# The third block pair of an FFN's up projection: its transposes directly behind the early products

## The chip, the cores and the metric

The kernel runs on one core of a Trainium2 chip. The metric is device time in microseconds (us) of one execution; lower is better. The program is a whole forward pass: four layers, one launch.

## The reference

A trunk of four layers on an input of 256 tokens x 1024 channels, all in float32. Each layer is a token mixer (kinds A, B, C, A) and then a gated FFN with a causal convolution over three tokens; each of the two is normed before and after and added to the residual. Cut to what matters here:

```python
def conv_ffn(h, w_up, conv_w, conv_b, w_down):
    u = h @ w_up                                   # 256 x 1024 by 1024 x 5632
    up = jnp.pad(u, ((0, 0), (CONV_WIDTH - 1, 0), (0, 0)))
    c = conv_b + up[:, CONV_WIDTH - 1:] * conv_w[CONV_WIDTH - 1]
    for j in range(CONV_WIDTH - 1):
        c = c + up[:, j:j + S] * conv_w[j]
    gate, val = jnp.split(c, 2, axis=-1)           # 2816 columns each
    return (jax.nn.gelu(gate, approximate=True) * val) @ w_down

def reference(x, ...):
    h = x
    for i in range(DEPTH):
        y = mixer_of_kind(i % 3)(rms_norm(h, g[0]))
        h = h + rms_norm(y, g[1])
        y = conv_ffn(rms_norm(h, g[2]), ...)
        h = h + rms_norm(y, g[3])
    return h
```

## The kernel before

**Products.** Every float32 operand is split into a rounded high part and a rest, and each product is made of three TensorE matmuls (`mm3`, lines 315 to 317): high x high, high x rest, rest x high. The weights come in units of 128 x 1024 values. `next_unit` takes one: SyncE starts its DMA into a `raw` tile (four buffers), ScalarE (ACT) copies it to the high part `wh` (line 277), VectorE (DVE) subtracts to give the rest `wl` (line 278). There are six `wh`/`wl` buffers, so ACT and DVE run up to six units ahead of TensorE (PE) and then wait for PE to be done with a buffer.

**The up projection of the FFN.** `w_up` is cut into 22 pairs of column blocks (`NFF`), the i-th pair being 128 gate columns and the 128 value columns that belong to them. One pair is two units. What is wanted in PSUM for a pair is columns on the partitions and tokens along the row, 128 x 256 for the gate and the same for the value, because the convolution then is a shift along the row.

- Pairs 3 to 21 are made that way directly by `proj`: the weights are the stationary operand, the transposed activations `yT` the moving one, 24 matmuls of 256 columns for each unit.
- Pairs 0 to 2 are made early and the other way round (`early`, line 459), since the first 128 tokens of `yT` are there before the last 128: `yT` is stationary, the weights move, and the result has tokens on the partitions. For the first token half, then for the second: pairs 0 and 1 go into the tile `early` (512 columns), ACT copies it to SBUF (`tok`, line 470), and pair 2 goes into the tile `more`, which the trace calls `up`. Behind the last product of the half, PE turns `tok` with four 128 x 128 transposes (line 474) into the tiles of pairs 0 and 1. Between the halves stands `late()`, eight transposes of the second token half (`zT`, line 429).
- `turn` (line 476) does the rest for pair 2: ACT copies `more` to a `tok` tile of its own (line 481), and PE turns it with four transposes (line 486) into a tile `turn`.

`activate` (its first instruction is line 1205, on ACT) does convolution, gelu and product of a pair, ACT and DVE alternating. It runs behind the products: it is recorded when more than three pairs wait in the list `behind`.

**What sets the order.** Each engine runs its instructions in a fixed order. A scheduler makes it from its own estimate of times, keeping to data dependences and to `issue_after(x)`, which makes what is recorded inside it stand behind x on the engine's queue. In `early`, `issue_after(last)` puts the four transposes somewhere behind the last early product of the half; in `ffn`, `turn` is called after the first unit of pair 3 and its transposes stand behind that unit's last product. `early` and `turn` are also used in mixers B and C, through `proj_pair`, with other blocks behind them. A wait of an engine is decided by semaphores when the instruction is at the head of its queue: everything behind it on that engine waits too.

Of the kernel before, what the change touches and what calls it, by code (L numbers as in the profile page):

```python
# [19 lines left out]
P = 128  # L20
D = 1024
KB = D // P
S = 256
# [203 lines left out]
class Trunk:  # L227
# [231 lines left out]
    def early(self, yT, outs, late, more):  # L459


        nc = self.nc
        units = [self.next_unit() for _ in range(6)]
        both = [self.ps_ot(f"early{self.unit}_{t}") for t in range(2)]
        for t in range(2):
            if t == 1:
                late()
            self.proj_tok(TILES[t], both[t], yT, units[:4], 2)
            tok = self.work.tile([P, 512], F32, tag="z", bufs=2, name=f"tok{self.unit}_{t}")
            nc.scalar.activation(tok, both[t], AF.Copy)  # L470
            last = self.proj_tok(TILES[t], more[:, t * S : (t + 1) * S], yT, units[4:])
            with self.tc.issue_after(last.ins):
                for n in range(4):
                    nc.tensor.transpose(outs[n][:, t * P : (t + 1) * P], tok[:, n * P : (n + 1) * P], self.ident)

    def turn(self, more, n, after):

        nc = self.nc
        tok = self.work.tile([P, 512], F32, tag="z", bufs=2, name=f"tok{self.unit}")
        tok = tok[:, : 2 * n * P].rearrange("p (t n) -> p t n", t=2)  # L480
        nc.scalar.activation(tok, more.rearrange("p (t n) -> p t n", t=2)[:, :, : n * P], AF.Copy)
        out = self.ps_tr(f"turn{self.unit}")
        with self.tc.issue_after(after.ins):
            for t in range(2):
                for j in range(n):
                    nc.tensor.transpose(out[:, j * S + t * P : j * S + (t + 1) * P], tok[:, t, j * P : (j + 1) * P], self.ident)
        return out

    def rows_mm(self, y, xT, unit, half, start, stop):
# [704 lines left out]
    def ffn(self, yT, L, finish, late):  # L1194
        nc = self.nc
        with self.tc.tile_pool(name="ffn", bufs=1) as fp:
# [3 lines left out]
            def activate(i, ps):  # L1200
                c = fp.tile([P, 2, S], F32, tag="c", bufs=2, name=f"c{L}_{i}")
                for j in range(2):
                    u = ps[:, j * S : (j + 1) * S]
                    w = [cw[:, i, j, k : k + 1] for k in range(4)]
                    nc.scalar.activation(c[:, j], u, AF.Identity, bias=w[3], scale=w[2])  # L1205
                    for k in (1, 0):
                        n = 2 - k
                        nc.vector.scalar_tensor_tensor(  # L1208
                            c[:, j, n:], in0=u[:, : S - n], scalar=w[k], in1=c[:, j, n:], op0=ALU.mult, op1=ALU.add
                        )  # L1210
                g = fp.tile([P, S], F32, tag="g", bufs=2, name=f"g{L}_{i}")
                nc.scalar.activation(g, c[:, 0], AF.Gelu_apprx_tanh)
                nc.vector.tensor_tensor(g, g, c[:, 1], op=ALU.mult)
                self.split(act[0][:, i], act[1][:, i], g)

            tiles = [self.ps_mm(f"up{L}_{i}") for i in range(2)]
            more = self.ps_one(f"up{L}_2")
            self.early(yT, [x[:, j * S : (j + 1) * S] for x in tiles for j in range(2)], late, more)
            self.prefetch(fp)
            behind = [(i, tiles[i]) for i in range(2)]  # L1220
            for i in range(3, NFF):
                ps = (self.ps_tr, self.ps_one, self.ps_ot, self.ps_ot, self.ps_mm, self.ps_mm, self.ps_tr, self.ps_tr)[i - 3 if i < 5 else 2 + (i - 5) % 6](f"up{L}_{i}")
                for j in range(2):
                    last = self.proj(ps[:, j * S : (j + 1) * S], yT, self.next_unit())
                    if i == 3 and j == 0:
                        behind.append((2, self.turn(more, 2, last)))
                behind.append((i, ps))
                while len(behind) > ACT_LAG:
                    activate(*behind.pop(0))
# [4 lines left out]
            def part(t, k, unit, half):  # L1234
                x = [a[:, k, t * P : (t + 1) * P] for a in act]
                return self.rows_mm(y[t], x, unit, half, k == 0, k == NFF - 1)
# [7 lines left out]
            for t in range(2):  # L1244
                with ExitStack() as ctx:
                    if t == 1:
                        ctx.enter_context(self.tc.issue_after(last.ins))
                    for k, half in halves(0, HOLD):
                        if t == 1 and k == HOLD - TAIL and half == 0 and self.turned:
                            ctx.enter_context(self.tc.issue_after(self.turned.ins))  # L1250
                        last = part(t, NFF - HOLD + k, units[k], half)
# [105 lines left out]
```

## Time and profile before

| | us |
|---|---|
| runs of before | 1600.68, 1596.98, 1599.86 |
| their median | 1599.86 |
| the profiled execution | 1599.39 |
| its span | 1597.6 |

| engine | busy us | share of the span | instructions |
|---|---|---|---|
| PE (matmul) | 1549.1 | 97% | 11016 |
| PEld (weight load) | 1444.8 | 90% | 11016 |
| DVE | 1213.1 | 76% | 2151 |
| ACT | 978.5 | 61% | 1707 |
| POOL | 252.7 | 16% | 310 |

The span is the time from the first to the last instruction of the profiled execution; its own time, 1599.39, lies 1.8 us above the span and 0.47 below the median. The mean granted clock of TensorE is 0.986 of its full speed. PE and PEld are two halves of one engine: the weight load of the next product runs beside the current product. Products overlap each other too, so a busy share of PE counts time in which at least one is under way, and the speed of PE is read from the distance between the starts of two products rather than from the duration of one.

### The profile page before, as it was taken

What the parts mean: (1) busy time and instruction counts of PE and PEld (TensorE: products, weight loads), DVE (VectorE), ACT (ScalarE), POOL (GpSimd) and SP (SyncE); (2) the same over time, 40 slices, a digit from 0 to 9 for tenths busy, and PEclk for the clock granted to TensorE, in tenths of its full rate; (3) what the DMA queues carried; (4) which work ended last, traced back from release to release, by engine and by line L of the source; (5) the groups of instructions that cost most, each with busy time, mean ns of one, the idle gap of its engine ahead of it and who ended that gap; (6) DMA issues with size and microseconds to landing.
All of it is one profiled execution on the core that took longest, in us unless ns stands there. A gap on an engine that the chain in (4) does not pass through costs nothing.

```text
span 1597.6 us, 29196 instructions
## 1 busy us (share of the span) xinstructions
PE 1549.1 (97%) x11016; PEld 1444.8 (90%) x11016; DVE 1213.1 (76%) x2151; ACT 978.5 (61%) x1707; POOL 252.7 (16%) x310
## 2 busy tenths in 40 slices
PE   7999999899999899999997999999999999899998
PEld 6999999799988789998886789988999999799986
DVE  5787898698856868885688679876587889779863
ACT  5566666476645847664567667655566666667642
POOL 2433321000001610000113200000443322000000
PEclk9999999899999999999997999999999999999999
DMA  7665556366574536557553066666556665556652
GB/s 259 198 183 180 181 183 204 122 217 189 177 238 144 146 110 221 187 171 246 170 185 101 10 202 192 188 186 211 171 178 187 180 183 178 167 185 195 187 189 79
DMA packets 103724, 282.73 MB, mean 177 GB/s; under 512 B 10928, under 2 KB 40112, under 8 KB 103584
## 3 DMA queue, kind: packets, MB, share of 16 engines
q1 hardware_dynamic: 101376, 272.86, 54.8%
q0 software_dynamic: 2208, 8.01, 1.5%
q8 instruction: 87, 1.43, 0.4%
q14 instruction: 53, 0.43, 0.1%
HBM read 279.66 MB, written 1.16 MB: 176 GB/s over the span
## 4 chain that ended last, share of the span: by engine, by line
PE 85%; DVE 5%; issue 4%; ACT 3%; DMA 2%; POOL 1%; SPq 0%; DVEq 0%; POOLq 0%; ACTq 0%
PE up L315 10%; PE up L317 9%; PE up L316 9%; PE qk L315 5%; PE qk L317 5%; PE qk L316 5%; PE y_ff L315 5%; PE y_ff L317 5%; PE y_ff L316 5%; PE s L858 4%; PE v L317 3%; PE v L316 3%; PE v L315 3%; PE pT L531 2%; DMA raw<-in_weights_dram 2%
## 5 line engine op out<-in xcount | busy, mean ns | idle before, releaser
L277 ACT ACTIVATE wh<-raw 128x1024 fp32r<-128x1024 f32 x473 | 495.5, 1057 | 357.2 <-PE up L316 124.1
L278 DVE TENSOR_TENSOR wl<-raw,wh 128x1024 fp32r<-128x1024 f32 x433 | 534.1, 1242 | 169.5 <-ACT wh L277 167.1
L315 PE MATMUL up<-yT,wh 128*128 128x256 f32 x1216 | 340.4, 280 | 0.0
L316 PE MATMUL up<-yT,wh 128*128 128x256 f32 x1216 | 339.9, 280 | 0.0
L317 PE MATMUL up<-yT,wl 128*128 128x256 f32 x1216 | 339.3, 279 | 0.0
L317 PEld LDWEIGHTS up<-yT,wl 128*128 128x128 f32 x1216 | 228.6, 188 | 0.0
L315 PEld LDWEIGHTS up<-yT,wh 128*128 128x128 f32 x1216 | 228.3, 188 | 0.0
L316 PEld LDWEIGHTS up<-yT,wh 128*128 128x128 f32 x1216 | 227.4, 187 | 0.0
L315 PE MATMUL qk<-yT,wh 128*128 128x256 f32 x768 | 216.1, 281 | 0.0
L316 PE MATMUL qk<-yT,wh 128*128 128x256 f32 x768 | 215.9, 281 | 0.0
L317 PE MATMUL qk<-yT,wl 128*128 128x256 f32 x768 | 215.8, 281 | 0.0
L1208 DVE SCALAR_TENSOR_TENSOR c<-up,cw,c 128x255 f32<-128x255 f32 x336 | 156.2, 477 | 5.1 <-ACT c L1205 2.5
L315 PEld LDWEIGHTS qk<-yT,wh 128*128 128x128 f32 x768 | 144.8, 188 | 2.3 <-issue 1.5
L316 PEld LDWEIGHTS qk<-yT,wh 128*128 128x128 f32 x768 | 144.8, 189 | 1.6 <-issue 0.7
L317 PEld LDWEIGHTS qk<-yT,wl 128*128 128x128 f32 x768 | 144.6, 188 | 1.5 <-issue 0.7
L315 PE MATMUL y_ff<-wh,act 128*128 128x512 f32 x352 | 138.1, 394 | 0.0
L317 PE MATMUL y_ff<-wh,act 128*128 128x512 f32 x352 | 138.0, 392 | 0.0
L376 POOL TENSOR_TENSOR r_post<-v_post,neg_half 128x1 f32<-128x1 f32 x16 | 8.9, 554 | 811.5 <-DVE v_post L374 811.5
L316 PE MATMUL y_ff<-wl,act 128*128 128x512 f32 x352 | 136.8, 389 | 0.0
L278 POOL TENSOR_TENSOR wl<-raw,wh 128x1024 fp32r<-128x1024 f32 x40 | 97.7, 2442 | 174.7 <-ACT wh L277 143.4
L315 PE MATMUL v<-wh,yT 128*128 128x256 f32 x400 | 113.7, 286 | 0.3 <-ACT yT L432 0.2
L316 PE MATMUL v<-wl,yT 128*128 128x256 f32 x400 | 113.7, 285 | 0.2 <-DVE wl L278 0.2
(233 smaller groups left out, 3086.8 us busy)
## 6 DMA issues: line engine op xcount, KB each, us to landing
raw<-in_weights_dram SPq DMA_DIRECT2D x473, 512.0 KB, 4.3
bias<-rows SPq DMA_DIRECT2D x160, 128.0 KB, 3.7
gain<-in_norm_gains_dram POOLq DMA_DIRECT2D x15, 512.0 KB, 4.8
out_dram<-h SPq DMA_DIRECT2D x2, 512.0 KB, 2.6
h<-in_x_dram SPq DMA_DIRECT2D x2, 256.0 KB, 3.5
gain<-in_norm_gains_dram SPq DMA_DIRECT2D x1, 512.0 KB, 5.7
h<-in_x_dram SPq DMA_DIRECT2D x1, 512.0 KB, 9.8
onehot<-in_onehot_dram SPq DMA_DIRECT2D x1, 448.0 KB, 11.4
```

The source lines that it names most:

```text
L277: self.nc.scalar.activation(hi, src, AF.Copy)
L278: (engine or self.nc.vector).tensor_tensor(lo, src, hi.bitcast(F32), op=ALU.subtract)
L315: mm(out, lh, rh, start=start, stop=False)
L316: mm(out, lh, rl, start=False, stop=False)
L317: return mm(out, ll, rh, start=False, stop=stop)
L376: self.p_last = nc.gpsimd.tensor_tensor(r, v, self.neg_half, op=ALU.pow)
L531: nc.tensor.transpose(ps[:, i * P : (i + 1) * P], x, self.ident)
L858: self.s_last = self.nc.tensor.matmul(out, q, k, start=start, stop=stop)
L1208: nc.vector.scalar_tensor_tensor(c[:, j, n:], in0=u[:, : S - n], scalar=w[k], in1=c[:, j, n:], op0=ALU.mult, op1=ALU.add)
```

## The change

`early` returns its last product. In `ffn`, `turn` is called right behind `early` instead of after the first unit of pair 3, so its transposes need only stand behind the last early product. `turn` keeps its last transpose, and all products of pairs 3 to 7 are put behind that transpose with `issue_after`. Mixers B and C call the same helpers as before.

```diff
--- before.py
+++ after.py
@@ -472,6 +472,7 @@
             with self.tc.issue_after(last.ins):
                 for n in range(4):
                     nc.tensor.transpose(outs[n][:, t * P : (t + 1) * P], tok[:, n * P : (n + 1) * P], self.ident)
+        return last
 
     def turn(self, more, n, after):
 
@@ -483,7 +484,7 @@
         with self.tc.issue_after(after.ins):
             for t in range(2):
                 for j in range(n):
-                    nc.tensor.transpose(out[:, j * S + t * P : j * S + (t + 1) * P], tok[:, t, j * P : (j + 1) * P], self.ident)
+                    self.turn_last = nc.tensor.transpose(out[:, j * S + t * P : j * S + (t + 1) * P], tok[:, t, j * P : (j + 1) * P], self.ident)
         return out
 
     def rows_mm(self, y, xT, unit, half, start, stop):
@@ -1215,15 +1216,17 @@
 
             tiles = [self.ps_mm(f"up{L}_{i}") for i in range(2)]
             more = self.ps_one(f"up{L}_2")
-            self.early(yT, [x[:, j * S : (j + 1) * S] for x in tiles for j in range(2)], late, more)
+            last = self.early(yT, [x[:, j * S : (j + 1) * S] for x in tiles for j in range(2)], late, more)
             self.prefetch(fp)
             behind = [(i, tiles[i]) for i in range(2)]
+            behind.append((2, self.turn(more, 2, last)))
             for i in range(3, NFF):
                 ps = (self.ps_tr, self.ps_one, self.ps_ot, self.ps_ot, self.ps_mm, self.ps_mm, self.ps_tr, self.ps_tr)[i - 3 if i < 5 else 2 + (i - 5) % 6](f"up{L}_{i}")
                 for j in range(2):
-                    last = self.proj(ps[:, j * S : (j + 1) * S], yT, self.next_unit())
-                    if i == 3 and j == 0:
-                        behind.append((2, self.turn(more, 2, last)))
+                    with ExitStack() as ctx:
+                        if i < 8:
+                            ctx.enter_context(self.tc.issue_after(self.turn_last.ins))
+                        self.proj(ps[:, j * S : (j + 1) * S], yT, self.next_unit())
                 behind.append((i, ps))
                 while len(behind) > ACT_LAG:
                     activate(*behind.pop(0))
```

Behind line 474 the lines of the changed kernel have numbers higher by one (486 is now 487, 481 is 482, 1205 is 1206).

What this does to the order of the instructions. First PE in the FFN of layer 0 before, around the end of the early products; `up_2` is the tile of pair 2, `up_3` that of pair 3, `yT` the transposed activations, `tok` ACT's copy of an early tile. Where a row of dots stands, 9 and then 16 more products of `up_3` are left out:

```order
L316 MATMUL up_2_3780<-wl_3814,yT_0_2_3662 128x256
L317 MATMUL up_2_3780<-wh_3813,yT_0_2_3663 128x256
L315 MATMUL up_3_3945<-yT_0_2_3662,wh_3948 128x256
L316 MATMUL up_3_3945<-yT_0_2_3663,wh_3948 128x256
L317 MATMUL up_3_3945<-yT_0_2_3662,wl_3949 128x256
...
L315 MATMUL up_3_3945<-yT_0_2_3662,wh_3948 128x256
L474 MATMUL up_0_3778<-ident,tok_1_3911 128x128 x2
L474 MATMUL up_1_3779<-ident,tok_1_3911 128x128 x2
L316 MATMUL up_3_3945<-yT_0_2_3663,wh_3948 128x256
...
L315 MATMUL up_3_3945<-yT_0_2_3662,wh_3985 128x256
L486 MATMUL turn_3978<-ident,tok_3976 128x128 x4
L316 MATMUL up_3_3945<-yT_0_2_3663,wh_3985 128x256
```

Before, 13 products of `up_3` stand between the last early product and the transposes of line 474, and 18 more between these and the transposes of `turn`. The same place on PE in the changed kernel:

```order
L316 MATMUL up_2_3780<-wl_3814,yT_0_2_3662 128x256
L317 MATMUL up_2_3780<-wh_3813,yT_0_2_3663 128x256
L474 MATMUL up_0_3778<-ident,tok_1_3911 128x128 x2
L474 MATMUL up_1_3779<-ident,tok_1_3911 128x128 x2
L487 MATMUL turn_3947<-ident,tok_3945 128x128 x4
L315 MATMUL up_3_3952<-yT_0_2_3662,wh_3955 128x256
L316 MATMUL up_3_3952<-yT_0_2_3663,wh_3955 128x256
L317 MATMUL up_3_3952<-yT_0_2_3662,wl_3956 128x256
```

Both groups of transposes now stand directly behind the last early product, and the 31 products stand behind both. It is the same in the FFN of all four layers. Next ACT at this place, before:

```order
L277 ACTIVATE wh_4028<-raw_4026 128x1024
L470 ACTIVATE tok_1_3911<-early_1_3818 128x512
L277 ACTIVATE wh_4058<-raw_4056 128x1024
L277 ACTIVATE wh_4101<-raw_4099 128x1024
L481 ACTIVATE tok_3976<-up_2_3780 128x512
L277 ACTIVATE wh_4131<-raw_4129 128x1024
L1205 ACTIVATE c_0_4013<-up_0_3778,cw 128x256
```

And in the changed kernel:

```order
L277 ACTIVATE wh_4028<-raw_4026 128x1024
L470 ACTIVATE tok_1_3911<-early_1_3818 128x512
L277 ACTIVATE wh_4058<-raw_4056 128x1024
L277 ACTIVATE wh_4101<-raw_4099 128x1024
L482 ACTIVATE tok_3945<-up_2_3780 128x512
L277 ACTIVATE wh_4131<-raw_4129 128x1024
L1206 ACTIVATE c_0_4013<-up_0_3778,cw 128x256
```

Nothing moved here: the copy that `turn` needs stands behind the same two weight copies. The queues of POOL and SyncE are in the same order as before. The scheduler has also moved a few products in mixers B and C, which the source does not touch; the largest such place is on PE in mixer B (`s` are scores, `pt` the turned probabilities, `ot` the product with the values, `pT` transposes of probabilities). Before:

```order
L858 MATMUL s_6_1_6607<-kd,q 128x256
L858 MATMUL s_6_1_6607<-kl,q 128x256
L858 MATMUL s_6_1_6607<-kd,q 128x256
L858 MATMUL s_6_1_6607<-kl,q 128x256
L316 MATMUL ot_2_6419<-pt_1_5858,v 128x256
L317 MATMUL ot_2_6419<-pt_0_5857,v 128x256
L315 MATMUL ot_2_6419<-pt_0_5857,v 128x256
L316 MATMUL ot_2_6419<-pt_1_5858,v 128x256
L317 MATMUL ot_2_6419<-pt_0_5857,v 128x256
L555 MATMUL pT_3_1_6504<-ident,p_3_1_6392 128x128 x3
```

In the changed kernel:

```order
L316 MATMUL ot_2_6419<-pt_1_5858,v 128x256
L317 MATMUL ot_2_6419<-pt_0_5857,v 128x256
L315 MATMUL ot_2_6419<-pt_0_5857,v 128x256
L316 MATMUL ot_2_6419<-pt_1_5858,v 128x256
L317 MATMUL ot_2_6419<-pt_0_5857,v 128x256
L556 MATMUL pT_3_1_6504<-ident,p_3_1_6392 128x128 x3
L859 MATMUL s_6_1_6607<-kd,q 128x256
L859 MATMUL s_6_1_6607<-kl,q 128x256
L859 MATMUL s_6_1_6607<-kd,q 128x256
L859 MATMUL s_6_1_6607<-kl,q 128x256
```

Four score products moved behind five products with the values and three transposes. Two more places, one in mixer B (`s_7_1`) and one in mixer C (six products of `s_3`), have moves of the same kind.

## Rows read from the trace of the kernel before

**Rows 1.** The page: span, and the chain that ended last, by engine.

```profile
span 1597.6 us, 29196 instructions
...
PE 85%; DVE 5%; issue 4%; ACT 3%; DMA 2%; POOL 1%; SPq 0%; DVEq 0%; POOLq 0%; ACTq 0%
```

**Rows 2.** Windows: us, busy and (count) of PE, PEld, DVE, ACT, POOL; clock, DMA share, GB/s.

```profile
322.00:328.00 6.00, 6.00 (x55) 6.00 (x54) 5.13 (x7) 5.54 (x8) 0.00 (x0) 1.00 0.80 276
```

**Rows 3.** Timeline of PE, layer 0: start us, duration us, engine, line, operation, out<-in, count.

```profile
322.92 0.28 PE L317 MATMUL up<-wh,yT 128*128 128x256 f32 x1
...
324.39 0.28 PE L315 MATMUL up<-yT,wh 128*128 128x256 f32 x1
324.51 0.60 PE L474 MATMUL up<-ident,tok 128*128 128x128 f32 x4
...
327.07 0.60 PE L486 MATMUL turn<-ident,tok 128*128 128x128 f32 x4
327.43 0.36 PE L316 MATMUL up<-yT,wh 128*128 128x256 f32 x1
327.63 0.28 PE L317 MATMUL up<-yT,wl 128*128 128x256 f32 x1
...
330.10 0.28 PE L317 MATMUL up<-yT,wl 128*128 128x256 f32 x1
```

**Rows 4.** Timeline of ACT, layer 0; in brackets idle time before it and its releaser.

```profile
321.81 0.60 ACT L470 ACTIVATE tok<-early 128x512 f32<-128x512 f32 x1 [0.40 <-PE early L317]
322.30 2.00 ACT L277 ACTIVATE wh<-raw 128x1024 fp32r<-128x1024 f32 x2
324.20 0.59 ACT L481 ACTIVATE tok<-up 128x512 f32<-128x512 f32 x1
```

**Rows 5.** Timelines, layer 3: the last early product on PE, and ACT's copy.

```profile
1421.50 0.28 PE L317 MATMUL up<-wh,yT 128*128 128x256 f32 x1
...
1422.78 0.59 ACT L481 ACTIVATE tok<-up 128x512 f32<-128x512 f32 x1
```

**Rows 6.** Timelines and a window: transposes and a short wait in the early part, layer 0.

```profile
312.84 0.60 PE L474 MATMUL up<-ident,tok 128*128 128x128 f32 x4
313.28 1.04 PE L429 MATMUL zT<-ident,z_pre 128*128 128x128 f32 x8
314.56 0.50 PE L315 MATMUL early<-wh,yT 128*128 128x512 f32 x1 [0.25 <-ACT yT L432]
...
312.00:316.00 4.00, 3.75 (x28) 3.34 (x27) 2.25 (x4) 1.09 (x2) 1.10 (x2) 1.00 0.32 101
```

**Rows 7.** Timelines of ACT and PE and a window: PE waits for ACT in mixer C.

```profile
914.42 0.42 ACT L277 ACTIVATE oT<-o 128x256 fp32r<-128x256 f32 x1 [0.49 <-DVE o L571]
...
914.88 0.50 PE L315 MATMUL y_o<-wh,oT 128*128 128x512 f32 x1 [1.38 <-ACT oT L277]
...
914.00:918.00 4.00, 3.12 (x14) 2.57 (x15) 1.50 (x3) 1.30 (x4) 0.00 (x0) 1.00 0.00 0
```

**Rows 8.** Timeline of PE and a window: a longer wait in mixer C.

```profile
873.46 1.51 PE L549 MATMUL ot<-pt,v 128*128 128x256 f32 x4 [1.76 <-ACT p L509]
...
873.40:877.00 3.60, 3.54 (x12) 3.11 (x13) 2.48 (x12) 1.67 (x6) 1.61 (x2) 0.53 0.72 265
```

**Rows 9.** Timeline of PE: first and last of 16 products at the lower clock.

```profile
528.79 0.42 PE L858 MATMUL s<-kd,q 128*128 128x256 f32 x1
...
531.99 0.35 PE L858 MATMUL s<-kd,q 128*128 128x256 f32 x1
```

**Rows 10.** Waits of PE: waiting <- waited for: us in total, times, longest us.

```profile
PE ot L549 <- DVE pt L278: 1.6, 4, 0.8
```

**Rows 11.** Timeline of PE, mixer A of layer 0: products behind transposes.

```profile
19.35 1.04 PE L429 MATMUL zT<-ident,z_pre 128*128 128x128 f32 x8
...
20.46 0.28 PE L317 MATMUL v<-wh,yT 128*128 128x256 f32 x1
...
30.89 0.28 PE L316 MATMUL v<-wl,yT 128*128 128x256 f32 x1
```

## Prediction

> **What bounds the kernel now.** I read the page first. The chain of work that ended last is 85% PE; DVE, ACT and waits for DMA share the rest [rows 1]. So the question is whether PE stands still, or how fast it goes, at the place of the change. The second view is a window over the end of the early products and the start of pair 3 in layer 0: PE is busy for 6.00 of 6.00 us at a clock of 1.00, ACT for 5.54, DVE for 5.13 [rows 2]. No engine but PE is the bound there, but ACT has little room: whatever PE needs from ACT at once, it gets only when ACT has worked off what stands ahead of it. The third view, PE's timeline, gives the pace. The last early product starts at 322.92. The 13 products of `up_3` that follow come at a distance of (324.39 - 322.92) / 13 = 0.113 us; the transposes of line 474 start at 324.51, those of `turn` at 327.07, with the 31st product just ahead; the 33rd starts at 327.63, and from there the distance is (330.10 - 327.63) / 21 = 0.1176 us [rows 3]. None of these rows has a bracket: PE waits for nothing there. The fourth view, ACT's timeline, tells why. ACT copies the early tile (line 470) at 321.81, then two units of weights in 2.00 us, and only at 324.20 the tile of pair 2 (line 481), done at 324.20 + 0.59 = 324.79 [rows 4]. Before, `turn` comes to that copy at 327.07, 2.28 us after it ended. That slack is what the 31 products buy.
>
> **What the change costs.** It adds and removes no work: the same four transposes twice, the same copies, the same products, no DMA more or less. The queues of POOL and SyncE keep their order, and so does ACT's at this place. What moves is PE's queue alone: both groups of transposes pass in front of 31 products.
>
> 1. The transposes of line 474 now start one step behind the last early product, at 322.92 + 0.11 = 323.03. Their source was copied by 321.81 + 0.60 = 322.41, so they don't wait. Four transposes followed by other transposes take 313.28 - 312.84 = 0.44 us [rows 6]: PE comes to `turn` at 323.47.
> 2. `turn` needs ACT's copy, which ends at 324.79. It can't come sooner: the two weight copies still stand ahead of it, and these ran without a gap [rows 4], so nothing in the change shifts them. From an end on ACT to a start on PE it takes 914.88 - (914.42 + 0.42) = 0.04 us [rows 7]. `turn` starts at 324.83, and **PE stands still for 324.83 - 323.47 = 1.36 us**. Everything behind it on PE waits too, because products of pairs 3 to 7 are now bound to stand behind it; their weights are long converted, and nobody else is helped by the pause.
> 3. From the start of `turn` to the next product it takes 327.43 - 327.07 = 0.36, to the one after 0.20 [rows 3]. So the first product of `up_3` starts at 325.19, the second at 325.39, and the 33rd, at the slower distance, at 325.39 + 31 x 0.1176 = 329.04.
> 4. Before, the 33rd started at 327.63. **PE is 1.41 us later.** This already includes what is saved: PE goes over from products to transposes and back once instead of twice.
>
> Can anything win it back? ACT and DVE get the tiles of pairs 0 and 1 earlier, at 323.47 instead of 324.95, so `activate` of pair 0 may begin sooner. That helps no one: PE does not wait in this stretch [rows 2], so an engine that gets ahead is off the path. What ends late is PE itself, and the start of the down projection and of the next layer move with it.
>
> Layer 3 has the same distances: from the last early product to the end of the copy it is 1422.78 + 0.59 - 1421.50 = 1.87 us, in layer 0 324.79 - 322.92 = 1.87 [rows 3 to 5]. The order of the queues is the same in all four FFNs, so I take the cost four times: 4 x 1.41 = 5.6 us. Made against the profiled execution: 1599.39 + 5.6 = **1605.0**. The median of the runs is 0.47 above that execution, which I leave aside.
>
> **Bounds of the unknown.** The wait itself isn't in the trace of before. Its low end: ACT takes the copy the moment the last early product has landed, at 322.92 + 0.28 = 323.20; it ends at 323.79, `turn` starts at 323.83, the wait is 0.36 instead of 1.36, and the cost 0.41 a layer: 1.6 us in all, 1601.0. ACT's order speaks against it. I take the upper value, since it stands in rows of this very place. The high end comes from the clock. A wait of 1.38 us in mixer C leaves it at 1.00 in the window around it [rows 7]; one of 1.76 us is followed by 0.53 [rows 8]. Mine, 1.36, is nearest to the first, so I take no fall. What a fall costs: 16 products at the lower level (1.2 GHz) take 531.99 - 528.79 = 3.20 us for 15 distances [rows 9], at the full one (2.4 GHz) 15 x 0.1176 = 1.76, so 1.4 us each time. In the mixers the scheduler moved products at three places; a product with the values waited for DVE there for 0.8 us at most [rows 10], which may come or go at each: up to 2.4 us either way, and I take nothing, since the products moved have no less work around them than before.
>
> A rule speaks against the change here. Transposes are work for PE's queue, but are they for the clock? In the early part PE goes from 312.84 to 314.56 with 12 transposes and a wait of 0.25 and no other product, 1.72 us in all, and the clock is 1.00 in the window around it [rows 6]. That is nearly as long as the wait of 1.76 that was followed by a lower clock, so the row says that transposes hold the clock up. The Trainium skill, "TensorE: Matmul & The Clock Gate", section "Part 4: PE-mode transpose", says that a transpose does not count as PE-busy the same way as a product does. By that rule the time from 323.03 to 325.19 would all be idle for the clock, 0.44 + 1.36 + 0.36 = 2.16 us. By the row it is 1.36 only, and the sum stays at 1605.0; by the rule it would be the first rival's.
>
> **The rivals.**
>
> *The clock falls in every FFN.* Place: the first products of `up_3`. For it: 2.16 us without a product, longer than the 1.76 that cost the clock [rows 8]. Against it: the 1.36 of real standstill and the transposes that held it [rows 6, 7]. Price 1.4 a layer more: 1605.0 + 4 x 1.4 = 1610.6. Chance 0.08.
>
> *The products fall into the quicker rhythm, and the kernel gets faster.* Products of 256 columns run at 0.113 or at 0.1176 us on the same clock. In layer 0 they are quick until the transposes cut into them and slow behind them [rows 3]. That transposes need not do this is seen in mixer A: directly behind eight of them 92 products run from 20.46 to 30.89, 0.1134 each [rows 11]. If what sets the slow rhythm is a cut in the middle of a tile's products, the change, which has no such cut, leaves all 912 products of pairs 3 to 21 (19 pairs x 2 units x 24) quick. They win 912 x 0.0043 = 3.9 us a layer, against 1.4 lost: 1599.39 - 4 x 2.5 = 1589.4. It decides from 1.41 / 0.0043, about 330 quick products a layer, on. Against it: `up_3` now starts directly behind the very transposes that stood ahead of the slow stretch, and the step that follows them, 0.36 and 0.20, need not change. With three or four quick layers it is faster; chance 0.08. With one or two it is 5.6 - 3.9 or 5.6 - 7.8: 1601.1 or 1597.2, no difference that can be told.
>
> *The wait is mostly hidden.* The copy goes earlier than I think, 1601.0, or the quick rhythm comes in one or two layers. Together 0.12.
>
> That the change doesn't do what it says is ruled out by the order of PE's queue, where the transposes stand where they were to be.
>
> **How the numbers follow.** A measurement of this kernel tells about 0.2% from no change, 3.2 us: between 1596.7 and 1603.1 is the same. My forecast, a pause of 1.36 us in each of four layers, has 0.72. Slower is that and the clock's rival, 0.80; faster 0.08; the same 0.12. The range goes down to 1601.0, the early copy, and up to 1609.0, which holds a clock that falls in two or three of the four layers, or the mixers' 2.4 us above the forecast. It leaves out the quick rhythm in two layers and more and the clock's fall in all four, less than 2 in 10 together.
>
> **What the profile after would show.** If I am right: in all four FFNs one wait of PE of about 1.4 us at the transposes of line 487, released by ACT's copy at line 482, 5.4 us in all in the list of waits; the first product of `up_3` 2.2 to 2.3 us behind the last early one; 0.1176 us between products as before; a clock of 1.00 around; and the other stages as long as before. Wrong would be: no such wait (then ACT's copy came early), a clock near 0.5 behind the wait (the first rival), products at 0.113 us over hundreds of products (the second), or a wait of PE before that is gone elsewhere, which I see no place for.

## The result and the profile after

The changed kernel took 1610.54 us (median of 5 runs, 1606.03 to 1615.21) against 1599.27 for the kernel before (5 runs, 1596.96 to 1600.68). The ratio is 1.0056, 95% interval 1.0037 to 1.0074: slower by 9.0 us, 5.9 to 11.8. Run a second time beside other kernels it was slower by 10.1 us (ratio 1.0063, 1.0048 to 1.0078). The direction is the one that was forecast; the forecast of 5.6 us explains somewhat more than half of it.

The profiled execution took 1610.54 us with a span of 1608.8. PE's timeline at the end of the early products in layer 0, which answers to [rows 3]:

```profile
323.79 0.28 PE L317 MATMUL up<-wh,yT 128*128 128x256 f32 x1
323.90 0.60 PE L474 MATMUL up<-ident,tok 128*128 128x128 f32 x4
325.71 0.66 PE L487 MATMUL turn<-ident,tok 128*128 128x128 f32 x4 [1.21 <-ACT tok L482]
326.12 0.36 PE L315 MATMUL up<-yT,wh 128*128 128x256 f32 x1
326.33 0.28 PE L316 MATMUL up<-yT,wh 128*128 128x256 f32 x1
...
329.98 0.28 PE L317 MATMUL up<-yT,wl 128*128 128x256 f32 x1
```

ACT's timeline there, which answers to [rows 4]:

```profile
322.69 0.60 ACT L470 ACTIVATE tok<-early 128x512 f32<-128x512 f32 x1 [0.40 <-PE early L317]
323.18 1.99 ACT L277 ACTIVATE wh<-raw 128x1024 fp32r<-128x1024 f32 x2
325.08 0.58 ACT L482 ACTIVATE tok<-up 128x512 f32<-128x512 f32 x1
```

The copy ends at 325.08 + 0.58 = 325.66, `turn` starts at 325.71, and PE has stood still for 1.21 us ahead of it. From the last early product to the 33rd of `up_3` (the row at 329.98) it takes 6.19 us; before it was 327.63 - 322.92 = 4.71 [rows 3]. That is **1.48 us a layer**, forecast 1.41. The distance in layers 1 and 2 is 6.19 too, in layer 3 it is 6.14: 5.9 us for the four. PE's list of waits has one new line and one that has grown a little:

```profile
PE turn L487 <- ACT tok L482: 4.8, 4, 1.2
...
PE s L859 <- DVE nm L509: 2.9, 6, 0.8
```

The clock did not fall in the FFNs. Windows from the last early products on, in layers 0 and 1 (columns as in [rows 2]); layers 2 and 3 read 1.00 too:

```profile
323.50:330.00 6.50, 5.29 (x46) 5.05 (x46) 5.20 (x8) 4.90 (x7) 0.00 (x0) 1.00 0.83 256
606.90:613.50 6.60, 5.39 (x47) 5.16 (x46) 5.48 (x8) 5.11 (x8) 0.00 (x0) 1.00 0.80 268
```

So four pauses account for 5.9 us (3 x 1.48 + 1.43), and some 3 to 4 us are left. Cut at the first early product of each mixer's and each FFN's projection, the two profiled executions of the change show where they lie (us of each stage, from PE's timeline; "mixer A" is layer 0's, the one of layer 3 stands with the FFN before it):

| | mixer A | FFN 0 | mixer B | FFN 1 | mixer C | FFN 2 and mixer A | FFN 3 |
|---|---|---|---|---|---|---|---|
| before | 304.4 | 188.2 | 90.2 | 188.7 | 157.2 | 474.3 | 187.1 |
| changed | 305.3 | 189.7 | 93.8 | 190.3 | 159.1 | 473.8 | 189.2 |
| changed, second time | 305.7 | 189.7 | 91.6 | 190.9 | 159.1 | 474.2 | 189.2 |

Not all of this comes from the change: mixer A of layer 0, which ends ahead of the first instruction that differs on PE, is longer by 0.9 and 1.3 us too. Mixer C is longer by 1.9 us both times, but it took 159.2 us as well in a kernel that keeps its order of before (l23, below).

Mixer B is longer by 3.6 and 1.4 us. The source touches neither its code nor its data. In the first profile the place is a stretch in the middle of it. The kernel before, PE's timeline at a wait of 2.37 us and the windows of the stretch that begins there:

```profile
541.62 0.39 PE L316 MATMUL ot<-pt,v 128*128 128x256 f32 x1 [2.37 <-DVE pt L278]
...
545.43 0.52 PE L858 MATMUL s<-kd,q 128*128 128x256 f32 x1 [0.40 <-DVE nm L508]
...
541.60:545.00 3.40, 3.38 (x17) 3.00 (x17) 2.29 (x7) 2.09 (x5) 3.27 (x6) 0.61 0.95 203
545.00:548.00 3.00, 2.60 (x16) 2.16 (x16) 3.00 (x8) 1.68 (x7) 2.71 (x5) 0.87 1.03 392
548.00:551.00 3.00, 3.00 (x27) 2.91 (x24) 2.57 (x12) 2.74 (x11) 2.03 (x6) 1.00 0.66 209
```

The changed kernel behind the same wait:

```profile
545.00:548.00 3.00, 3.00 (x16) 3.00 (x16) 1.44 (x4) 1.53 (x3) 3.00 (x6) 0.50 0.95 256
548.00:551.00 3.00, 2.17 (x9) 1.81 (x8) 2.49 (x7) 2.12 (x8) 2.48 (x4) 0.50 0.82 328
551.00:554.00 3.00, 3.00 (x14) 2.71 (x13) 1.10 (x4) 0.61 (x3) 0.00 (x0) 0.54 0.77 213
554.00:557.00 3.00, 3.00 (x26) 2.90 (x25) 2.34 (x10) 2.04 (x7) 2.10 (x6) 1.00 0.09 26
```

And PE's timeline in it:

```profile
544.38 0.58 PE L316 MATMUL ot<-pt,v 128*128 128x256 f32 x1 [2.37 <-DVE pt L278]
...
549.42 0.55 PE L859 MATMUL s<-kd,q 128*128 128x256 f32 x1 [0.83 <-DVE nm L509]
```

Before, the lower clock (1.2 GHz) lasts 3.4 us, from about 542.4 to 545.8. Changed, it lasts some 10 us, from 543.5 to 553.8, and in the middle of it PE waits again, 0.83 us instead of 0.40, for the maxima of the softmax on DVE. The longer wait comes with what the scheduler moved: DVE's and PE's orders in mixer B are not those of before.

The second profiled execution of the change has the same orders and the same two waits, but not the longer stretch at the lower clock. PE's timeline there at the second wait, then mixer B as a whole in windows before, changed and changed the second time:

```profile
549.06 0.36 PE L859 MATMUL s<-kd,q 128*128 128x256 f32 x1 [0.93 <-DVE nm L509]
...
495.00:587.00 92.00, 84.26 (x529) 74.38 (x528) 63.24 (x145) 58.80 (x144) 32.13 (x63) 0.96 0.47 135
495.00:587.00 92.00, 83.78 (x516) 74.76 (x515) 60.34 (x141) 58.61 (x144) 32.42 (x63) 0.93 0.43 118
495.00:587.00 92.00, 83.49 (x526) 74.05 (x525) 62.35 (x142) 58.71 (x144) 32.38 (x63) 0.96 0.44 124
```

The granted clock is 0.96, 0.93 and 0.96. At the clock of before, then, the new order makes mixer B 1.4 us longer. The whole second execution took 1609.69 us, 10.3 more than the one of before, at a mean clock of 0.987 against 0.986, so a loss of this size needs no lower clock. The first execution had the longer stretch at the lower clock besides. That the second wait made it is not shown: the lower clock had lasted some 5 us (543.5 to 548.6) when that wait began.

### The profile page after: what moved, and what is told of

Its sections match the earlier page's. It is cut to its first block, busy times and chain, and to the rows that moved or that the text cites. A ratio compares the mean times of both kernels' runs of the same rounds, so it can differ in the third digit from the quotient of the medians.

```text
span 1608.8 us, 29202 instructions
## 1 busy us (share of the span) xinstructions
PE 1554.9 (97%) x11016; PEld 1450.0 (90%) x11016; DVE 1215.2 (76%) x2151; ACT 980.1 (61%) x1707; POOL 253.6 (16%) x310
## 3 DMA queue, kind: packets, MB, share of 16 engines
q8 instruction: 87, 1.43, 0.4%
## 4 chain that ended last, share of the span: by engine, by line
PE 56%; DVE 4%; ACT 3%; issue 2%; DMA 1%; POOL 0%; DVEq 0%; POOLq 0%; ACTq 0%
PE up L316 7%; PE up L315 7%; PE up L317 7%; PE y_ff L315 4%; PE y_ff L317 4%; PE y_ff L316 3%; PE qk L315 3%; PE qk L317 3%; PE qk L316 3%; PE s L859 2%; PE v L315 2%; PE v L317 2%; PE v L316 2%; DVE wl L278 1%; PE ot L550 1%
## 5 line engine op out<-in xcount | busy, mean ns | idle before, releaser
L1209 DVE SCALAR_TENSOR_TENSOR c<-up,cw,c 128x255 f32<-128x255 f32 (+1 forms) x336 | 157.3, 478 | 9.3 <-ACT c L1206 6.6
```

The source lines that it names most:

```text
L1209: nc.vector.scalar_tensor_tensor(c[:, j, n:], in0=u[:, : S - n], scalar=w[k], in1=c[:, j, n:], op0=ALU.mult, op1=ALU.add)
```

## The experiments

Each kernel ran beside the kernel before on the same chip. The difference in us is the ratio's, from about 1600. Because the mean granted clock differs from run to run, the last two columns part the difference of the mean times in two, as an estimate: mean time x mean clock (what would be left at full clock, if PE were busy all the time), and the rest, the clock's part. The estimate is rough: by the spread of the runs each part is sure to some 2 or 3 us only, and in the first row +3.6 us stand at full clock where the rows show four pauses of 5.9 us in all.

| kernel | runs | ratio, 95% interval | us | at full clock | the clock's part |
|---|---|---|---|---|---|
| changed, second time | 6 | 1.0063, 1.0048 to 1.0078 | +10.1 | +3.6 | +5.4 |
| layers 2 and 3 only (l23) | 12 | 1.0009, 0.9997 to 1.0021 | +1.4 | +4.9 | -3.4 |
| layer 0 only (l0) | 12 | 1.0031, 1.0017 to 1.0045 | +5.0 | +2.0 | +2.6 |
| layers 1 to 3 (l123) | 12 | 1.0032, 1.0019 to 1.0046 | +5.1 | +5.3 | +0.3 |
| ACT's copy first (copyfirst) | 12 | 1.0006, 0.9993 to 1.0020 | +1.0 | +0.8 | +0.1 |
| products not held (free) | 12 | 0.9997, 0.9984 to 1.0010 | -0.5 | +0.1 | -0.2 |
| changed, mixer B's order held (bfix) | 12 | 1.0038, 1.0026 to 1.0050 | +6.1 | +5.7 | -0.2 |
| before, scores moved (mixmove) | 12 | 1.0004, 0.9989 to 1.0020 | +0.6 | -0.6 | +0.6 |
| before, scores and DVE moved (mixdve) | 12 | 1.0004, 0.9990 to 1.0018 | +0.6 | 0.0 | +0.6 |
| before, one product more (extra512) | 12 | 0.9993, 0.9978 to 1.0007 | -1.1 | +0.9 | -1.4 |

**Is it the pause?** Two kernels take it away without undoing the change.

copyfirst puts ACT's copy for `turn` ahead of the weight copies of the units that follow:

```diff
-        nc.scalar.activation(tok, more.rearrange("p (t n) -> p t n", t=2)[:, :, : n * P], AF.Copy)
+        copy = nc.scalar.activation(tok, more.rearrange("p (t n) -> p t n", t=2)[:, :, : n * P], AF.Copy)
+        self.copied = (self.unit + 3, copy.ins)
...
+            if self.copied and self.copied[0] <= u < self.copied[0] + 3:
+                ctx.enter_context(self.tc.issue_after(self.copied[1]))
```

> The full change, with ACT's copy for the turn put ahead of the two weight copies. Theory P: the pause shrinks from 1.2 to 0.3 us by the rows, since the copy starts when the last early product has landed: 0.3 to 0.5 us a layer, 1.2 to 2 us in all, plus what the moved products in mixers B and C cost here (their order differs from the full change, 0 to 5 us): 1600.5 to 1606. Theory C: the pauses are too short to slow what follows: at most +2 us. If the pauses were no cause at all: +11 us as with the full change.

Measured: +1.0 us (-1.1 to +3.2). Its timelines in layer 0, first ACT's copy and the two weight copies, then PE:

```profile
322.96 0.60 ACT L485 ACTIVATE tok<-up 128x512 f32<-128x512 f32 x1 [0.82 <-PE up L320]
323.45 2.00 ACT L278 ACTIVATE wh<-raw 128x1024 fp32r<-128x1024 f32 x2
...
322.76 0.60 PE L477 MATMUL up<-ident,tok 128*128 128x128 f32 x4
323.61 0.66 PE L491 MATMUL turn<-ident,tok 128*128 128x128 f32 x4 [0.25 <-ACT tok L485]
324.02 0.36 PE L318 MATMUL up<-yT,wh 128*128 128x256 f32 x1
```

The copy starts when the last early product has landed and the pause is 0.25 us. The distance to the 33rd product is 5.23 us in all four layers, 0.52 more than before, so 2.1 us in all. PE's order in the FFN is the changed one to the row, and 9 of the 10 us are gone. They are not the pauses alone: mixer B has nearly its order of before in this kernel, its longer wait of the scores is missing, and it took 90.4 us.

free keeps the turn's own constraint and drops the hold on the products:

```diff
-                    with ExitStack() as ctx:
-                        if i < 8:
-                            ctx.enter_context(self.tc.issue_after(self.turn_last.ins))
-                        self.proj(ps[:, j * S : (j + 1) * S], yT, self.next_unit())
+                    self.proj(ps[:, j * S : (j + 1) * S], yT, self.next_unit())
```

> The turn directly behind the early products by its own constraint, as in the change, but the products of pairs 3 to 7 are not held behind it. The scheduler then fills PE's queue with products until ACT's copy is there; mixer B keeps its order of before. Theory P: no pause, so no loss: 0 +- 1.5 us, no row of PE waiting for tok. Rival (the turn's early place itself costs, by what ACT and DVE do earlier): +3 us or more.

Measured: -0.5 us (-2.6 to +1.6), and no line for `turn` in PE's list of waits. The scheduler puts 2 products ahead of the transposes of line 474 and some 30 ahead of `turn`:

```profile
325.35 0.60 PE L474 MATMUL up<-ident,tok 128*128 128x128 f32 x4
...
329.21 0.60 PE L487 MATMUL turn<-ident,tok 128*128 128x128 f32 x4
```

Mixers B and C have PE's, ACT's and DVE's orders of before. So the half of the change that moves the turn's own constraint costs nothing; the half that holds the products, with what the scheduler moves because of it, is the loss. Nothing in the data asks for the hold, and without it the products are the cover that the copy needs.

**Does every layer cost the same?** The change in some layers only, by a condition on the layer's number in `ffn` (`CHANGED` is (2, 3) in l23, (0,) in l0, (1, 2, 3) in l123):

```diff
+CHANGED = (2, 3)
...
+            now = L in CHANGED
+            if now:
+                behind.append((2, self.turn(more, 2, last)))
...
-                        if i < 8:
+                        if i < 8 and now:
...
+                    if i == 3 and j == 0 and not now:
+                        behind.append((2, self.turn(more, 2, last)))
```

> The change in the FFNs of layers 2 and 3 only; layers 0 and 1 as before. No product of mixers B and C changes its place. Theory P (each early turn costs its pause, about 1.45 us, and the rest of the 11 us comes from products that the scheduler moved in mixers B and C): 2 x 1.45 = +2.9 us, about 1602, mixers B and C as long as before. Theory C (what follows a pause is slower too, so that each of the four costs 11 / 4 = 2.8 us): +5.6 us, about 1605.

Measured: +1.4 us (-0.5 to +3.4). The 2.9 of theory P lies inside, the 5.6 of theory C outside.

> The change in the FFN of layer 0 only; the scheduler moves the same products of mixer B as in the full change, and some in mixer C. Theory P: 1.45 us for the pause and the whole of the mixers' part, about 5 us: +6 to +7, about 1606, with mixer B 2 to 3 us longer than before. Theory C: +2.8 us, about 1602.

Measured: +5.0 us (+2.7 to +7.2), three times a pause. One layer alone brings half of the whole loss. Its mixer B has the order of the full change and took 91.5 us, with the wait of the scores for DVE at 0.93 and the lower clock no longer than before.

> The change in the FFNs of layers 1, 2 and 3; layer 0 as before, and with it mixer B. Mixer C is in the order of the full change. Theory P+B: three pauses, 4.4 us, and nothing in mixer B: +4 to +5 us. Rival (each FFN costs a quarter of the full change's 10 us): +7.5 us.

Measured: +5.1 us (+3.0 to +7.4): three pauses are 4.4. The three layers together cost what layer 0 alone does. Mixer B took 90.2 us, as before. By these middle values the pause is about the same everywhere, and what is over hangs on layer 0's FFN, the only one ahead of mixer B; each is sure to some 2 us.

**Is it mixer B's order?** The full change once more, for a comparison with the next ones:

> The full change once more, next to the two kernels below. Theory P with the sizes seen so far: 4 pauses at 1.45 us = 5.8 us, and 2 to 4 us from the products moved in mixers B and C, as in the kernel with the change in layer 0 only (5.0 less 1.45): +8 to +10 us. If the first 11 us were mostly the spread of single runs: +5.8 us and no more.

Measured: +10.1 us (+7.7 to +12.5). Then the full change with three of DVE's orders in mixer B held as before:

```diff
...
+                with ExitStack() as ctx:
+                    if r == 5 and a == 1:
+                        ctx.enter_context(self.tc.issue_after(self.pt_lo[f"{L}_2_0"].ins))
+                    if r in (6, 7) and a == 0:
+                        ctx.enter_context(self.tc.issue_after(self.pt_lo[f"{L}_{r - 4}_1"].ins))
                     for t in range(2):
                         n = (t + 1) * P
                         self.exps(pp[t], s[:, t, :n], bias[:, 0, :n], st, 2 * a + t, own, n)
```

> The full change in all four FFNs, with three orders held in mixer B as they were before: the score exponents of pair 5 behind the turned probabilities of pair 2 on DVE, those of pairs 6 and 7 behind the probabilities of pairs 2 and 3. Theory P+B (the change costs its four pauses, 5.8 us, and 1 to 3.5 us in mixer B through DVE's order there): +6 to +8 us, and mixer B back at 90.0 to 90.5 us from 91.5 to 93.8. Rival (the surplus over the pauses does not come from mixer B's order): +10 us as with the full change.

Measured: +6.1 us (+4.2 to +8.0), about the four pauses (5.9); mixer B took 89.9 us. By the estimate in the table the clock's part has gone from +5.4 to -0.2. The order is not free of waits. PE's timeline from the same wait as above:

```profile
542.85 0.39 PE L317 MATMUL ot<-pt,v 128*128 128x256 f32 x1 [2.37 <-DVE pt L279]
...
546.64 0.36 PE L860 MATMUL s<-kd,q 128*128 128x256 f32 x1 [1.57 <-DVE nm L510]
```

The windows behind it:

```profile
543.00:546.20 3.20, 2.07 (x17) 1.83 (x17) 2.01 (x6) 2.80 (x8) 3.20 (x6) 1.00 0.98 298
546.20:549.20 3.00, 2.46 (x15) 1.97 (x15) 3.00 (x8) 1.14 (x5) 2.72 (x5) 1.00 0.86 288
```

The scores wait even longer here, 1.57 us, but the clock stays at 1.00, and the stage is as short as before. That need not be the doing of the held orders. Some 14 us earlier in mixer B both kernels have the same wait for POOL; behind it the clock fell before and did not fall in this execution. Before, then bfix:

```profile
527.30 0.55 PE L555 MATMUL pT<-ident,p 128*128 128x128 f32 x3 [2.26 <-POOL p L970]
527.30:532.20 4.90, 4.89 (x29) 4.90 (x30) 4.75 (x19) 4.26 (x12) 0.26 (x2) 0.65 0.77 226
...
528.85 0.55 PE L557 MATMUL pT<-ident,p 128*128 128x128 f32 x3 [2.26 <-POOL p L977]
528.80:532.20 3.40, 3.35 (x28) 3.36 (x29) 3.31 (x14) 2.72 (x9) 0.30 (x2) 1.00 0.83 264
```

So the 89.9 us were measured at a clock that mixer B did not have before, and this profile doesn't show what the held orders are worth. What the twelve runs show is that little or nothing is left over the pauses, -1.7 to +2.1 us.

The reverse, mixer B's new order in the kernel before, was tried in two steps. First the score products alone:

```diff
...
+                with ExitStack() as ctx:
+                    if r >= 6 and a == 1:
+                        ctx.enter_context(self.tc.issue_after(self.pT_at[f"{L}_{r - 3}_1"].ins))
+                    for t in range(2):
+                        self.qk(s[:, t], q[:, r, a, TILES[t]], kd[:, 0, a], kl[:, 0, a])
```

> The kernel before with one thing of the change that its source doesn't name: the score products s_6_1 and s_7_1 of mixer B stand where the scheduler puts them in the full change, behind three transposes of probabilities. The FFNs are as before. Theory P: this is the mixers' part, +2 to +4 us, with mixer B longer by it. Rival (the moved products cost nothing, and the surplus of the full change is a lower clock that follows from the pauses' shift in time): 0 +- 1.5 us.

Measured: +0.6 us (-1.8 to +3.2), mixer B 90.3 us: the moved score products cost nothing that shows. Then, with them, DVE's order of the second exponents:

```diff
...
                     n = (t + 1) * P
-                    self.exps(pp[t], s[:, t, :n], bias[:, 0, :n], st, 2 * a + t, own, n)
+                    with ExitStack() as ctx:
+                        if r >= 5 and a == 1 and t == 1:
+                            ctx.enter_context(self.tc.issue_after(self.pt_lo[f"{L}_{r - 3}_1"].ins))
+                        self.exps(pp[t], s[:, t, :n], bias[:, 0, :n], st, 2 * a + t, own, n)
```

> The kernel before, its FFNs untouched, with mixer B ordered as the scheduler orders it in the full change: the score products s_6_1 and s_7_1 as in the run that moved these alone, and on DVE the second score exponents of pairs 5, 6 and 7 behind the turned probabilities of pairs 2, 3 and 4. A few orders of the full change on ACT and of single products are not taken over. Theory P+B (DVE's order in mixer B makes the next scores wait and costs 1.3 to 4 us): +1.5 to +4 us, mixer B at 91.5 us or more, a wait of about 0.9 us of the scores for DVE. Rival (mixer B's order is harmless, what was seen there was the clock): 0 +- 1.5 us, mixer B at 90.0 to 90.5.

Measured: +0.6 us (-1.6 to +2.9), mixer B 90.9 us, and the wait of 0.9 us for the maxima did not come. The lower clock lasted longer all the same, at least 6.0 us behind the wait of 2.36 us, as this window shows:

```profile
541.20:547.20 6.00, 5.97 (x25) 5.61 (x26) 4.89 (x13) 3.80 (x12) 5.87 (x10) 0.50 0.96 283
```

My theory fails here: these orders are not sufficient. What they leave out of the full change are the exponents of pair 5 in another sequence, three single products with the values, and the places of a few copies on ACT. Which of these makes the wait, or whether it takes a time shift as well, stays open. In l0, l123 and bfix the surplus comes and goes with mixer B's order as a whole; of it 1.3 to 1.4 us are seen in mixer B at the clock of before, and where the other 2 us lie is not shown.

**Can the quicker rhythm be had?** In the changed kernel all 910 distances of `up` products in each layer, from the second product behind the turn on, are at the slower pace, 0.1178 us on average; the second rival did not come. Three kernels looked for what sets it. The first puts one product of 512 columns behind the turn in the kernel before:

```diff
+        if extra is not None:
+            yT, hi = extra
+            with self.tc.issue_after(turned.ins):
+                nc.tensor.matmul(self.ps_one(f"extra{self.unit}"), yT[0][:, 0, :P], hi[:, :512], start=True, stop=True)
```

> The kernel before with one more product of 512 columns directly behind the transposes of turn, its result unused. Theory R (the slow rhythm of the products, 0.1176 us, is set by what stands directly ahead, and behind a 512-column product it is 0.113): 879 products a layer win 0.0043 us each, 3.8 us a layer, less 0.24 for the product: -14 us, about 1585. Rival (the rhythm does not hang on it): +0.24 a layer, +1 us, plus what the scheduler's other order in mixers B and C costs, 0 to 5 us: 1600 to 1606.

Measured: -1.1 us (-3.5 to +1.1), the products behind it at 0.1178 in all four layers. Theory R falls. The next adds a cut ahead of each of 16 pairs in each layer:

```diff
+    def cut(self, L, m, out, yT, hi):
+        mm = self.nc.tensor.matmul
+        if L == 0:
+            return mm(out[:, : 32 * (m + 1)], yT[0][:, 0, :P], hi[:, : 32 * (m + 1)], start=True, stop=True)
+        if L == 1:
+            return mm(out[:, : 16 * (m + 1)], hi[:, :P], yT[0][:, 0, : 16 * (m + 1)], start=True, stop=True)
...
```

> The kernel before with one cut of PE's stream ahead of each of the pairs 6 to 21 in every FFN: in layer 0 a product with 32, 64, ... 512 moving weight columns, in layer 1 one with 16, 32, ... 256 moving token columns, in layer 2 one to sixteen transposes, in layer 3 one to sixteen products of 512 columns; their results are unused. The time says nothing here (+20 to +40 us of added work); what is looked at is the distance of the 48 products behind each cut. Theory R2 (a cut of the right kind or length brings the 0.113 us rhythm): some of the 64 stretches at 0.113. Rival (the products of this form keep to 0.1176 once they are there): none.

Measured, in one profiled execution (1650.09 us with the added work): 63 of the 64 stretches at 0.1176 to 0.1179 us, one at 0.1133, behind the product of 512 columns in layer 0:

```profile
426.87 0.39 PE L1197 MATMUL extra<-wh,yT 128*128 128x512 f32 x1
427.10 0.28 PE L315 MATMUL up<-yT,wh 128*128 128x256 f32 x1
...
430.50 0.28 PE L315 MATMUL up<-yT,wh 128*128 128x256 f32 x1
```

The 30 products between the last two rows take 3.40 us, 0.1133 each. The third kernel repeats this cut in three forms and places:

```diff
+        if L in (0, 1):
+            return mm(out, yT[0][:, 0, :P], hi[:, 512 * L : 512 * L + 512], start=True, stop=True)
+        if L == 2:
+            return mm(out, hi[:, :P], yT[0][:, :2].rearrange("p k n -> p (k n)"), start=True, stop=True)
+        return mm(out, yT[0][:, m % KB, P:], hi[:, :512], start=True, stop=True)
```

> As the run on the rhythm, every cut now one product of 512 columns: layer 0 as the one cut that brought the 0.113 us distance (ahead of each pair from 6 on), layer 1 with the other half of the weights in the middle of each pair, layer 2 with 512 moving token columns, layer 3 with the other token half stationary. Theory R3 (such a product brings the quick rhythm): most of the 64 stretches at 0.113 us. Rival (the one quick stretch was chance, which products come out in which rhythm is not set by the form of the cut): few or none, without a pattern.

Measured: none of 64 stretches quick, the same cut at the same pair of layer 0 among them:

```profile
428.85 0.40 PE L1197 MATMUL extra<-wh,yT 128*128 128x512 f32 x1
429.08 0.28 PE L315 MATMUL up<-yT,wh 128*128 128x256 f32 x1
...
432.61 0.28 PE L315 MATMUL up<-yT,wh 128*128 128x256 f32 x1
```

The same 30 products take 3.53 us. Neither the form nor the place of the cut sets the rhythm. The transposes by themselves don't either, as a kernel from above shows. In layers 1 to 3 of free the products come at 0.1178 us ahead of the transposes of line 474 and are quick behind them, up to those of `turn`. PE's timeline in layer 1:

```profile
604.15 0.60 PE L474 MATMUL up<-ident,tok 128*128 128x128 f32 x4
604.51 0.36 PE L317 MATMUL up<-yT,wl 128*128 128x256 f32 x1
604.71 0.28 PE L315 MATMUL up<-yT,wh 128*128 128x256 f32 x1
...
607.77 0.28 PE L316 MATMUL up<-yT,wh 128*128 128x256 f32 x1
607.88 0.60 PE L487 MATMUL turn<-ident,tok 128*128 128x128 f32 x4
```

The 27 distances from 604.71 to 607.77 are 0.1133 us each. The steps behind the transposes, 0.36 and 0.20 us, are those that are followed by the slow rhythm in the kernel before [rows 3]. In layer 0 of free the products at this place are slow. What sets the rhythm is open.

No version beat the kernel before.

## Why the prediction was right, and by how much it fell short

- *What bounds the kernel.* Right. PE had no wait at this place before, so each pause went whole into the time; nothing behind it took it back. copyfirst, with the same order on PE in the FFN, lost 1.0 us instead of 10. One sentence was too wide: "What moves is PE's queue alone". Further on in each up projection the scheduler moved instructions of ACT and DVE too; it cost nothing there, since behind the early products PE's only wait in an FFN is the one for `tok`.
- *Steps 1 to 4, the pause.* Right in place, cause and size: `turn` waits for ACT's copy behind two weight copies in all four FFNs, 1.2 us by the row where 1.36 was forecast. The transposes, with a wait behind them, show as busy for longer, and the first two products follow `turn` at 0.41 and 0.21 us instead of 0.36 and 0.20. The whole is 1.48 us later where 1.41 was forecast: 5.9 against 5.6 us. That this is the cause of the larger part is shown by the removed pause (copyfirst), the removed hold (free) and the kernel in which little but the pauses is left (bfix, +6.1).
- *One assumption of step 2* doesn't hold every time: "it can't come sooner" was right, but it can come later. In the second profile of the change the second weight copy in layer 1 waited for its DMA, and the pause there is 1.81 us (ACT's timeline, then PE's):

```profile
607.00 1.06 ACT L277 ACTIVATE wh<-raw 128x1024 fp32r<-128x1024 f32 x1 [0.54 <-DMA raw<-in_weights_dram]
607.97 0.58 ACT L482 ACTIVATE tok<-up 128x512 f32<-128x512 f32 x1
...
608.60 0.66 PE L487 MATMUL turn<-ident,tok 128*128 128x128 f32 x4 [1.81 <-ACT tok L482]
```

The window around it:

```profile
606.00:610.00 4.00, 2.19 (x19) 1.95 (x19) 2.92 (x3) 3.46 (x6) 0.00 (x0) 1.00 0.66 208
```

- *The step that was mis-sized* is the mixers' term. I took nothing for the products that the scheduler moved there, "since the products moved have no less work around them than before", with 2.4 us either way as the bound. Measured, it is what is left of 9.0 and 10.1 us over the pauses of 5.9: 3 to 4 us, and bfix, with the pauses kept and mixer B's order held, is at +6.1. The wait that came is of the size that bounded it, 0.83 and 0.93 us where 0.40 stood before, at one place and for the scores instead of the products with the values. The forecast weighed only PE's order there; DVE's, on which this wait is, had moved too. Mixer B was 1.4 us longer with it at the clock of before, and 3.6 us in the execution with the longer stretch at the lower clock, a cost that the bound did not hold. The rest of the 3 to 4 us is not placed; of what the profiled executions add, 0.9 and 1.3 us lie in mixer A, ahead of the change.
- *The range.* The ratio of the first comparison puts the changed kernel at 1599.86 x 1.0056 = 1608.8, and the second run's median was 1608.85: just inside 1601.0 to 1609.0. The first median by itself, 1610.54, is above it. That the range held is in part luck: with the mixers' bound of 2.4 us alone it would have ended at 1607.4, and the room above that stood for a clock that falls in some FFNs, which none did.
- *The first rival*, the clock falling in each FFN, did not come. Its time, 1610.6, is where the first median lies, but for another reason: the clock is 1.00 in all four FFNs, and the longer fall was in mixer B.
- *The rule of the Trainium skill*, "TensorE: Matmul & The Clock Gate", "Part 4: PE-mode transpose", by which transposes don't count as PE-busy the same way, would have cost the clock here as the forecast read it. This case's rows don't agree with it as a rule for a whole stretch: from the last early product to the first of `up_3` there are 2.33 us with only 8 transposes and a pause, in one layer 2.94 us with a pause of 1.81, and the clock is 1.00 in the windows around them. That rule was rightly not put into the sum.
- *The second rival*, the quicker rhythm, did not come. The reason put against it, that the step behind the transposes need not change, does not decide it: in free the same steps are followed by quick products in three layers. That it stayed away is not explained.

## What to carry to other kernels

When a consumer is moved up in one engine's queue, look up where its producer stands in the other engine's queue: if that order stays, the move turns the cover into a pause, and the products that were held back were the cover. Put the copy first (here 9 of 10 us) or leave the products free (all of it), and count on the copy to come later still when a load ahead of it is late. Where a scheduler makes the orders, compare those of every engine in the stages that the source doesn't touch: here a third of the loss lies over the pauses, and with mixer B's order held (bfix) little or nothing of it was left. Before a stage's time in one profile is put down to an order, look whether its clock was that of the profile it is compared with.

## What the runs showed of the hardware

- The same wait was followed by the lower clock for very different times. Behind the wait of 2.37 us in mixer B it lasted 3.4 us before, in l0 and in the second execution of the change, at least 6.0 us in mixdve, some 10 us in the first execution of the change, and did not come in bfix. A second wait does not account for it: it was 0.93 us in l0 and in the second execution, 1.57 us in bfix and missing in mixdve. The length of a wait by itself did not tell either: 1.81 us left the clock at 1.00 in layer 1.
- Products of 256 columns on the same clock ran at 0.1133 or 0.1178 us each and kept to one of the two, to the slower for hundreds of products. Behind 128 cuts of many forms they became quick once, and the same cut in the same place did not do it again. Behind four transposes quick products went on slow in the kernel before, and slow ones went on quick in three layers of free.
- The mean granted clock of whole runs differs from kernel to kernel by some us' worth: l23, with two pauses, came out at only +1.4 us; its runs had a higher mean clock (0.9902 against 0.9880), which by the estimate in the table is 3.4 us.
